# Feed-forward layers by seven block products in place of eight, with gated products through DRAM

## The chip, the cores and the metric

One core of a Trainium2 chip runs the whole program. TensorE (PE in the profile) multiplies; VectorE (DVE), ScalarE (ACT) and GpSimd (POOL) work elementwise; SyncE (SP) issues the DMAs. The metric is the device time of one execution in microseconds (us), as the median of three runs.

## The reference, cut to what matters

Two layers over a sequence of 1024 tokens with 1024 features: a mixer (RWKV-7 in layer 0, mLSTM in layer 1), each followed by a gated feed-forward network of width 2816, with modulated norms before both and a last norm behind everything.

```python
D_FF = -(-(8 * D_MODEL) // (3 * 256)) * 256      # 2816

def _swiglu(x, w_gu, w_down):
    gu = x @ w_gu
    return (jax.nn.silu(gu[..., :D_FF]) * gu[..., D_FF:]) @ w_down

    for i in range(DEPTH):
        ...
        x = x + g1 * y                            # y: the mixer
        h = _rms(x) * (1.0 + sc2) + sh2
        x = x + g2 * _swiglu(h, ffn_w_gu[i], ffn_w_down[i])
    return _rms(x) * final_w
```

## The kernel before, in words

Features lie on partitions, tokens along the free axis. The 1024 tokens are two halves of 512, so a stream is 8 tiles of 128x512 for each half: `x[0]` and `x[1]`. Every large operand is split into two parts (`split`): a rounded copy `hi` on ACT and the rest `lo = src - hi` on DVE; a product of two 128-blocks is then three matmuls (hi hi, hi lo, lo hi), each 128x128 against 128x512 (`dense`).

In a feed-forward layer `gu` makes one of 22 tiles of the gated product: 24 matmuls with the gate's weights, Silu on ACT, 24 with the up weights, a multiplication on DVE, and a split. The 22 tiles go in five groups (`GROUPS`), since SBUF does not hold all of them; after each group `down` multiplies it by its rows of the second weight matrix and adds the result, times the gate `mod`, to `x`. That is 22 x 2 x 24 x 2 + 8 x 2 x 66 = 3168 matmuls in a layer.

`ffn_open` does the first group of the first half, `ffn_rest` the others. The first half's first group runs beside the last steps of RWKV's state chain (`c` banks, one step of 64 tokens after the other), and the work of one half stands beside the norm of the other: after the projection of `x[1]` (`project`), its norm (`rstd`, `normed`) runs while PE does the rest of the first half's `down`. In layer 1 the projection of `x[0]` runs beside the last mLSTM steps. A norm is: squares on ACT, their sum on DVE, a sum over partitions on PE (`sc<-kc,mt`), a power on POOL (`rs`), a broadcast on PE (`sc<-kc,rs`), eight multiplications on DVE, eight scalings on ACT, eight splits.

All SBUF tiles of both mixers and the feed-forward layers come from one pool, `ROOM`, in which a tag has a number of rooms that the phases share. Instructions are ordered by a scheduler at build time: it puts them on each engine by priority (the program's order, moved forward by `AHEAD`) and readiness; on the chip each engine then runs its list strictly in that order. All DMAs of weights and streams are issued by SP, in one list as well, and `background` slips steps of a side task (here the second layer's modulation, `ada`) between the weights.

## Time and profile before

| | us |
|---|---|
| median of 3 runs | 3158.77 (3158.58 to 3174.7) |
| profiled execution, its span | 3153.0 |
| PE busy | 3049.4 (97%) |
| DVE busy | 1611.2 (51%) |
| ACT busy | 1231.7 (39%) |
| POOL busy | 73.8 (2%) |
| moved by DMA | 323.14 MB, 102 GB/s over the span |

The profile describes one execution, whose span is the time from the first to the last record; the median of the runs is 5.8 us above it. Inside the span stand, in order: RWKV to about 1105 us, feed-forward layer 0 to about 1860, mLSTM to about 2310, feed-forward layer 1 to 3133, and the last norm.

### The profile page before, as it was taken

To read this page: it belongs to the slowest core of one execution; us is meant where nothing else is said; L and a number is where in the kernel's file an instruction comes from. 1 tells how busy PE (TensorE), PEld (TensorE's weight loads), DVE (VectorE), ACT (ScalarE), POOL (GpSimd) and SP (SyncE) were. 2 spreads that over 40 slices of the span, in tenths; PEclk is the share of its full clock that TensorE was granted. 3 is DMA by queue.
4 is the path that set the end of the run, shared out by engine and by line. 5 is a ranking of instruction groups with operands and counts; after the bars stand their busy time and mean duration, and the time that the engine had idled before them with its cause. 6 is when DMAs were issued, how large, how long until landed. Compare 5 with 4: busy or idle time off the path is not lost.

```text
span 3153.0 us, 44874 instructions
## 1 busy us (share of the span) xinstructions
PE 3049.4 (97%) x17656; PEld 2392.0 (76%) x17656; DVE 1611.2 (51%) x3238; ACT 1231.7 (39%) x2378; POOL 73.8 (2%) x97
## 2 busy tenths in 40 slices
PE   7899989999999999999999999999999999999998
PEld 5577767777777777888888877777778888888886
DVE  7867576776577555423334276333364432323225
ACT  6656675665655633211111144323343321111112
POOL 0000000000000000000000000000000000000000
PEclk9898688999889899999999999899999999999999
DMA  8764333344444243422122151011242321111113
GB/s 293 268 213 135 100 112 111 107 115 135 137 118 123 94 133 112 127 66 82 60 84 87 54 188 57 29 46 47 67 157 93 96 76 38 58 35 60 44 44 97
DMA packets 227656, 323.14 MB, mean 102 GB/s; under 512 B 110541, under 2 KB 113229, under 8 KB 227445
## 3 DMA queue, kind: packets, MB, share of 16 engines
q1 hardware_dynamic: 213620, 295.10, 30.5%
q10 hardware_dynamic: 13824, 25.17, 2.1%
q8 instruction: 139, 2.28, 0.3%
q14 instruction: 73, 0.59, 0.1%
HBM read 268.28 MB, written 51.90 MB: 102 GB/s over the span
## 4 chain that ended last, share of the span: by engine, by line
PE 85%; DVE 6%; issue 4%; ACT 2%; DMA 1%; POOL 1%; SPq 0%; POOLq 0%; DVEq 0%; ACTq 0%
PE dn L180 42%; PE c L180 30%; PE sc L180 4%; PE iv L180 4%; PE px L180 3%; PE tr L180 1%; PE tr L616 0%; DVE wlo L185 0%; DVE a L185 0%; POOL gv L775 0%; DVE KT L249 0%; PE tr L711 0%; POOL rs L299 0%; PE tr L1078 0%; ACT whi L184 0%
## 5 line engine op out<-in xcount | busy, mean ns | idle before, releaser
L180 PE MATMUL dn<-a,whi 128*128 128x512 f32 (+2 forms) x1656 | 593.0, 427 | 18.3 <-ACT a L184 6.7
L184 ACT ACTIVATE whi<-wraw 128x1024 fp32r<-128x1024 f32 (+2 forms) x254 | 238.4, 939 | 658.6 <-PE dn L180 344.5
L185 DVE TENSOR_TENSOR wlo<-wraw,whi 128x1024 fp32r<-128x1024 f32 (+2 forms) x254 | 272.2, 1072 | 336.8 <-ACT whi L184 333.6
L180 PEld LDWEIGHTS dn<-a,whi 128*128 128x128 f32 (+2 forms) x1656 | 316.8, 197 | 102.2 <-issue 11.2
L180 PE MATMUL dn<-a,wlo 128*128 128x512 f32 (+1 forms) x856 | 362.2, 426 | 7.0 <-ACT tmp L383 2.2
L180 PEld LDWEIGHTS dn<-a,wlo 128*128 128x128 f32 (+1 forms) x856 | 168.9, 198 | 48.2 <-issue 6.9
L184 ACT ACTIVATE VU<-wraw 128x1024 fp32r<-128x1024 f32 (+2 forms) x86 | 77.2, 897 | 293.4 <-PE dn L180 131.1
L180 PE MATMUL c<-a,whi 128*128 128x512 f32 (+1 forms) x536 | 168.3, 394 | 1.1 <-DVE a L185 1.1
L185 DVE TENSOR_TENSOR VU<-wraw,VU 128x1024 fp32r<-128x1024 f32 (+2 forms) x86 | 87.7, 1020 | 120.9 <-ACT VU L184 118.8
L180 PE MATMUL dn<-AR,whi 128*128 128x512 f32 (+1 forms) x392 | 123.6, 396 | 0.0
L180 PE MATMUL dn<-KT,whi 128*128 128x512 f32 (+1 forms) x392 | 123.0, 395 | 0.0
L180 PEld LDWEIGHTS c<-a,whi 128*128 128x128 f32 (+1 forms) x536 | 100.4, 188 | 26.0 <-issue 2.2
L180 PE MATMUL c<-a,wlo 128*128 128x512 f32 x272 | 107.6, 396 | 4.2 <-ACT a L184 4.2
L824 DVE TENSOR_TENSOR tmp<-dn,tmp 128x512 f32<-128x512 f32 x46 | 31.8, 691 | 145.9 <-PE dn L180 145.9
L180 PE MATMUL c<-a,VU 128*128 128x512 f32 x408 | 99.0, 396 | 0.0
L180 PE MATMUL dn<-a,VU 128*128 128x512 f32 (+1 forms) x408 | 97.8, 395 | 0.0
L180 PEld LDWEIGHTS sc<-AR,KB 64*128 64x128 f32 x512 | 74.7, 219 | 27.7 <-issue 13.7
L180 PE MATMUL sc<-AR,KB 64*128 64x128 f32 x512 | 89.4, 320 | 2.4 <-DVE KB L575 2.0
L180 PEld LDWEIGHTS c<-a,VU 128*128 128x128 f32 x408 | 76.2, 188 | 19.1 <-issue 1.1
L180 PEld LDWEIGHTS dn<-a,VU 128*128 128x128 f32 (+1 forms) x408 | 75.4, 185 | 19.6
L756 DVE SCALAR_TENSOR_TENSOR st<-st,dl,c 64x64 f32<-64x64 f32 x256 | 71.1, 278 | 34.3 <-PE c L180 29.7
L180 PE MATMUL c<-AR,whi 128*128 128x512 f32 x280 | 88.6, 397 | 0.0
(513 smaller groups left out, 6252.2 us busy)
## 6 DMA issues: line engine op xcount, KB each, us to landing
wraw<-in_wgu SPq DMA_DIRECT2D x108, 512.0 KB, 3.5
KT<-in_ada SPq DMA_DIRECT2D x40, 512.0 KB, 5.4
wraw<-in_wdn SPq DMA_DIRECT2D x64, 256.0 KB, 2.7
wraw<-in_wdn SPq DMA_DIRECT2D x48, 320.0 KB, 2.9
eb<-in_ada SPq DMA_DIRECT2D x48, 256.0 KB, 2.9
st<-in_ada SPq DMA_DIRECT2D x48, 256.0 KB, 2.7
wraw<-in_wk SPq DMA_DIRECT2D x16, 512.0 KB, 4.5
wraw<-in_wr SPq DMA_DIRECT2D x16, 512.0 KB, 4.3
```

The source lines that it names most:

```text
L180: return self.nc.tensor.matmul(out, lhsT, rhs, start=start, stop=stop, **kw)
L184: self.nc.scalar.activation(hi, src, AF.Copy)
L185: self.nc.vector.tensor_tensor(lo, src, hi.bitcast(F32), SUB)
L756: nc.vector.scalar_tensor_tensor(st[hs, hs], st[hs, hs], dl[hs, c:c + 1], p3[hs, hs], MUL, ADD)
L824: nc.vector.tensor_tensor(sil[i], ps, sil[i], MUL)
```

## The change

Both halves and both halves of the features make 2x2 blocks, and a block product of 2x2 by 2x2 blocks is made from seven products of blocks in place of eight (Winograd's form of Strassen's scheme: four sums of blocks ahead of the products on either side, seven sums behind).

- `seven` makes two tiles (n and n + 11) for both halves: 7 x 12 = 84 matmuls where 96 stood. Nine of eleven pairs go this way for gate and up; two (`NPLAIN`) stay plain. `wpair` loads the weights of two tiles, makes four sums on POOL, and splits seven blocks on ACT and DVE. Behind the products `seven` has three copies out of PSUM on ACT and four additions on DVE.
- `keep` makes four differences of the gated tiles on DVE and writes all seven to DRAM (`gd`, 256 KB each). After the last pair, `down` reads them back, splits them, and does the second matrix in seven products of 132 matmuls, in the order 1, 6, 7, 2, 4, 5, 3. Its weights' sums are made ahead by `sums` as a side task: 16 steps in a layer, each with 4 loads, 4 POOL additions of 128x352, and 4 stores. Layer 0 asks for seven steps of the side tasks in each `wpair` (`rate` 7), layer 1 for one.
- A layer has 2 x 2 x 2 x 2 x 24 + 9 x 2 x 84 + 7 x 132 = 2820 matmuls.
- SBUF is laid out anew per phase: `ROOM` for the mixers, `FROOM` for the feed-forward layers, over each other. A tile of the new phase waits for the tiles that lay in its place. Only `x` (8 rooms, `RES`) stays.
- The order of the halves' work changes with `ffn`: norm of `x[0]`, plain tiles of the first half, projection and norm of `x[1]` (in layer 1 the projection stands ahead of the plain tiles), plain tiles of the second half, the pairs, `down`.

```diff
+NH = 11
+NPLAIN = 2
...
-AHEAD = dict(chain=50, mask=400, w=50, finish=50)
+AHEAD = dict(chain=50, mask=400, w=50, finish=50, pair=100, g=150, norm=500)
+RES = {"x": (8, 520)}
...
+FROOM = {"wraw": (3, 1024), "wq": (8, 1024), "gb": (11, 1024), "ws": (3, 512), "tmp": (4, 512), "ga": (17, 1024),
+         "tt": (8, 512), "rs": (1, 4)}
...
+    def open(self, stack, rooms):
+        self.np += 1
+        for tag, (bufs, _) in rooms.items():
+            self.pools[tag] = stack.enter_context(
+                self.tc.tile_pool(name=f"{tag}_{self.np}", bufs=bufs, reuse_waits="tile"))
+        self.rooms_.update(rooms)
+    def phase(self, rooms=None):
+        if self.big is not None:
+            self.big.close()
+            self.rooms_ = dict(RES)
+            self.pools = {n: self.pools[n] for n in RES}
+        if rooms:
+            self.big = ExitStack()
+            self.open(self.big, rooms)
...
-    def gu(self, l, n, hs, gated):
-    def down(self, l, g, gated, x, which, ns=range(KT)):
-    def ffn_open(self, l, x, hs):
-    def ffn_rest(self, l, x, hs, gated, after):
...
+    def norm_blocks(self, xs, l, which):
+        nc = self.nc
+        r = self.rstd(xs)
+        for kt in range(KT):
+            nc.vector.tensor_tensor(xs[kt], xs[kt], r, MUL)
+            nc.scalar.activation(xs[kt], xs[kt], AF.Identity, scale=self.scp[l][:, 8 * which + kt:8 * which + kt + 1],
+                                 bias=self.mod[l][:, 24 * which + kt:24 * which + kt + 1])
+    def wpair(self, s1, s2):
+        nc = self.nc
+        self.background(self.rate)
+        out = {}
+        def part(n, src):
+            out[n] = self.two("wq")
+            self.split(*out[n], src)
+        with self.ahead("pair"):
+            r1, r2 = (self.t("wraw", [P, D]) for _ in range(2))
+            nc.sync.dma_start(r1, s1)
+            nc.sync.dma_start(r2, s2)
+            a11, a12, a21, a22 = r1[:, :HT], r1[:, HT:], r2[:, :HT], r2[:, HT:]
+            u, v, w = (self.t("ws") for _ in range(3))
+            add = nc.gpsimd.tensor_tensor
+            part(1, a11)
+            part(2, a12)
+            add(u, a21, a22, ADD)
+            add(v, u, a11, SUB)
+            part(6, v)
+            part(5, u)
+            add(a21, a11, a21, SUB)
+            part(7, a21)
+            part(4, a22)
+            add(w, a12, v, SUB)
+            part(3, w)
+        return out
...
+    def seven(self, w, X, tag):
+        nc = self.nc
+        def other():
+            return self.bank(self.alt("iv", "dn", "dn"))
+        def copy(ps):
+            t = self.t(tag)
+            nc.scalar.activation(t, ps, AF.Copy)
+            return t
+        a = self.bank(self.alt("c1", "c2", "px"))
+        self.product(a, w[1], X[1])
+        c11 = copy(a)
+        b = other()
+        self.product(b, w[2], X[2])
+        nc.vector.tensor_tensor(c11, b, c11, ADD)
+        self.product(a, w[6], X[6], start=False)
+        c12 = copy(a)
+        c = other()
+        self.product(c, w[5], X[5])
+        self.product(a, w[7], X[7], start=False)
+        c21 = copy(a)
+        c22 = self.t(tag)
+        nc.vector.tensor_tensor(c22, c, c21, ADD)
+        d = other()
+        self.product(d, w[4], X[4])
+        nc.vector.tensor_tensor(c21, d, c21, ADD)
+        self.product(c, w[3], X[3], start=False)
+        nc.vector.tensor_tensor(c12, c, c12, ADD)
+        return c11, c12, c21, c22
+    def keep(self, g, n, room):
+        nc = self.nc
+        g11, g12, g21, g22 = g
+        t2, t4, t3 = room
+        def put(i, t):
+            nc.sync.dma_start(self.gd[i - 1, n], t)
+        put(1, g11)
+        put(2, g21)
+        put(3, g22)
+        nc.vector.tensor_tensor(g12, g12, g11, SUB)
+        put(5, g12)
+        nc.vector.tensor_tensor(t2, g22, g12, SUB)
+        put(6, t2)
+        nc.vector.tensor_tensor(t4, g21, t2, SUB)
+        put(4, t4)
+        nc.vector.tensor_tensor(t3, t2, g11, SUB)
+        put(7, t3)
...
+    def sums(self, l):
+        nc = self.nc
+        w = self.A["wdn"]
+        k = NH * P
+        q = k // 4
+        add = nc.gpsimd.tensor_tensor
+        for n in range(4):
+            for c in range(0, k, q):
+                a11, a21, a22, a12 = (self.t("x", [P, q]) for _ in range(4))
+                for t, m, o in ((a11, n, 0), (a21, n + 4, 0), (a22, n + 4, k), (a12, n, k)):
+                    nc.sync.dma_start(t, w[l, m, :, o + c:o + c + q])
+                s1, s2 = (self.t("x", [P, q]) for _ in range(2))
+                add(s1, a21, a22, ADD)
+                add(s2, s1, a11, SUB)
+                add(a21, a11, a21, SUB)
+                add(a12, a12, s2, SUB)
+                for i, t in enumerate((s1, s2, a21, a12)):
+                    nc.sync.dma_start(self.wsd[i, n, :, c:c + q], t)
+                yield
...
+        to = {1: ((0, 0),), 6: ((0, 1),), 7: ((1, 0), (1, 1)), 2: ((0, 0),), 4: ((1, 0),), 5: ((1, 1),), 3: ((0, 1),)}
+        ps = [None] * 4
+        for i, p in enumerate((1, 6, 7, 2, 4, 5, 3)):
+            xs = []
+            for m in range(NH):
+                with self.ahead("g"):
+                    raw = self.t("tt")
+                    nc.sync.dma_start(raw, self.gd[p - 1, m])
+                    hi, lo = self.two("gb" if i % 2 else "ga")
+                    self.split(hi, lo, raw)
+                xs.append((hi, lo))
+            fresh = p in (1, 2, 4, 5)
+            def run(n, units, lo, first, last):
+                for u, w in enumerate(units):
+                    o = lo // P + 4 * u
+                    e = o + 4 if o + 4 <= NH else NH
+                    self.product(ps[n], w, xs[o:e], start=first and u == 0 and fresh, stop=last and u == len(units) - 1)
+            for n in range(4):
+                if fresh:
+                    ps[n] = self.bank(("c1", "c2", "px", "iv")[n])
+                run(n, weights(p, n, 0, D), 0, True, False)
+                if p != 1:
+                    run(n, weights(p, n, D, k), D, False, True)
+                    self.add_to(l, x, n, ps[n], to[p])
+            if p == 1:
+                for n in range(4):
+                    run(n, weights(p, n, D, k), D, False, True)
+                    self.add_to(l, x, n, ps[n], to[p])
+            if p == 4:
+                done(0)
+        done(1)
+    def add_to(self, l, x, n, ps, to):
...
+    def ffn(self, l, x, second, done, rate):
+        nc = self.nc
+        wgu = self.A["wgu"]
+        self.store(0, x[0])
+        self.norm_blocks(x[0], l, 1)
+        b11, b21 = self.parts(x[0][:4], "gb"), self.parts(x[0][4:], "gb")
+        if l == 1:
+            second()
+        g = {}
+        for n in range(NPLAIN):
+            for m in (n, n + NH):
+                g[m, 0] = self.plain(l, m, b11 + b21)
+        self.deep = True
+        if l == 0:
+            second()
+        self.store(1, x[1])
+        self.norm_blocks(x[1], l, 1)
+        b22 = self.parts(x[1][4:7], "gb") + self.parts(x[1][7:], "ga")
+        b12 = self.parts(x[1][:4], "ga")
+        for n in range(NPLAIN):
+            for m in (n, n + NH):
+                g[m, 1] = self.plain(l, m, b12 + b22)
+            self.keep((g[n, 0], g[n, 1], g[n + NH, 0], g[n + NH, 1]), n, [self.t("tmp") for _ in range(3)])
+        for kt in range(4):
+            f11, f21, f12, f22 = x[0][kt], x[0][kt + 4], x[1][kt], x[1][kt + 4]
+            nc.vector.tensor_tensor(f12, f12, f11, SUB)
+            nc.vector.tensor_tensor(f22, f22, f12, SUB)
+            nc.vector.tensor_tensor(f21, f21, f22, SUB)
+            nc.vector.tensor_tensor(f11, f22, f11, SUB)
+        X = {1: b11, 2: b21, 3: b22, 6: self.parts(x[1][4:], "ga"), 5: self.parts(x[1][:4], "ga"),
+             7: self.parts(x[0][:4], "ga"), 4: self.parts(x[0][4:], "ga")}
+        self.rate = rate
+        for n in range(NPLAIN, NH):
+            sil = self.seven(self.wpair(wgu[l, n], wgu[l, n + NH]), X, "tt")
+            for t in sil:
+                nc.scalar.activation(t, t, AF.Silu)
+            up = self.seven(self.wpair(wgu[l, NF + n], wgu[l, NF + n + NH]), X, "tmp")
+            for t, u in zip(sil, up):
+                nc.vector.tensor_tensor(t, u, t, MUL)
+            self.keep(sil, n, up[:3])
+        self.background(1000)
+        self.rate = 0
+        x[0] = self.load(self.rooms(0), 0, self.xd[0])
+        x[1] = self.load(self.rooms(1), 1, self.xd[1])
+        self.down(l, x, done)
...
-        # the first feed-forward layer
-        self.ng = 0
-        hs = {0: self.normed(x[0], 0, 1, self.a0)}
-        gated = self.ffn_open(0, x, hs)
+        self.phase(FROOM)
+        def second(y, w, l, tag):
+            x[1] = self.load(self.rooms(1), 1, None if l == 0 else self.xd[1])
+            run(self.project(y, w, l, x[1], lambda: self.two("ga"), tag))
+        self.bg = chain(self.sums(0), *(self.ada(s, HT, RAW1, "x") for s in (1, 0, 2, 4, 3, 5)))
+        self.ffn(0, x, lambda: second(self.yd[1], "wro", 0, ("tmp",)), lambda j: self.store(j, x[j]), 7)
+        self.phase(ROOM)
         self.deep = True
-        x[1] = self.load(self.rooms(1), 1)
-        run(self.project(self.yd[1], "wro", 0, x[1], self.a1, PB))
-        hs[1] = self.normed(x[1], 0, 1, self.a1)
...
-        self.bg, self.rate = chain(*(self.ada(s, HT, RAW1, "iv") for s in (1, 0, 2, 4, 3, 5))), 1
-        self.ffn_rest(0, x, hs, gated, after)
-        self.background(48)
-        # layer 1
-        self.deep = True
+        with self.ahead("norm"):
+            nh = {0: self.normed(x[0], 1, 0, self.a0)}
         self.ml_setup()
         ml = self.mlstm(nh)
         next(ml)
+        x[1] = self.load(self.rooms(1), 1, self.xd[1])
         nh[1] = self.normed(x[1], 1, 0, self.a1)
         next(ml)
-        spill(1)
         run(ml)
-        self.ng = 0
+        self.phase(FROOM)
         self.deep = True
-        x[0] = self.load(self.rooms(0), 0, xd[0])
-        run(self.project(self.yd[0], "wmo", 1, x[0], self.a0, PT))
-        hs = {0: self.normed(x[0], 1, 1, self.a0)}
-        x[1] = self.load(self.rooms(1), 1, xd[1])
-        run(self.project(self.yd[1], "wmo", 1, x[1], self.a1, PD))
-        gated = self.ffn_open(1, x, hs)
-        hs[1] = self.normed(x[1], 1, 1, self.a1)
-        self.ffn_rest(1, x, hs, gated, lambda i: self.final(i, x[i]))
+        x[0] = self.load(self.rooms(0), 0, self.xd[0])
+        run(self.project(self.yd[0], "wmo", 1, x[0], lambda: self.two("ga"), ("tmp",)))
+        self.bg = self.sums(1)
+        self.ffn(1, x, lambda: second(self.yd[1], "wmo", 1, ("tmp",)), lambda j: self.final(j, x[j]), 1)
+        self.phase()
```

Three places show what this does to the lists. First, PE at the end of RWKV's last state chain. `c` banks are the chain's, `dn` the feed-forward layer's. Before:

```order
L180 MATMUL c_2076_11240<-st_1458,AR_10437 128x128
L180 MATMUL dn_11566<-a_11346,whi_11562 128x512
L180 MATMUL dn_11566<-a_11345,wlo_11563 128x512
L180 MATMUL dn_11566<-a_11352,whi_11562 128x512
L180 MATMUL dn_11566<-a_11353,whi_11562 128x512
L180 MATMUL dn_11566<-a_11352,wlo_11563 128x512
L180 MATMUL dn_11566<-a_11359,whi_11562 128x512
L180 MATMUL c_2077_11243<-VU_11066,KT_10494 128x128
L180 MATMUL c_2076_11240<-VU_11066,SR_10449 64x64 x2
L180 MATMUL dn_11566<-a_11360,whi_11562 128x512
L180 MATMUL dn_11566<-a_11359,wlo_11563 128x512
L180 MATMUL dn_11566<-a_11366,whi_11562 128x512
```

and now (`sc` is the norm of `x[0]`, `tr` transposes of the finished heads):

```order
L208 MATMUL c_2076_11362<-st_1580,AR_10559 128x128
L208 MATMUL c_2077_11365<-VU_11188,KT_10616 128x128
L208 MATMUL c_2076_11362<-VU_11188,SR_10571 64x64 x2
L208 MATMUL sc_11516<-kc,tmp_11493 128x1 x4
L208 MATMUL c_2078_11372<-st_1580,AR_10559 128x128
L208 MATMUL sc_11524<-kc,rs_11521 128x128 x3
L208 MATMUL c_2079_11375<-VU_11188,KT_10616 128x128
L208 MATMUL c_2078_11372<-VU_11188,SR_10571 64x64 x2
L208 MATMUL sc_11524<-kc,rs_11521 128x128
L208 MATMUL dn_11570<-gb_11545,wq_11573 128x512 x2
L814 MATMUL tr_11406<-kc,Ys_11301 128x128
```

The chain's matmuls stand alone now; the first feed-forward matmul comes behind the chain and the norm.

Second, PE at the norm of `x[1]` in feed-forward layer 0 (`sc` is the norm). Before, `c` is a bank of `down` for the first half:

```order
L180 MATMUL c_2274_12227<-SA_11592,wlo_12224 128x512
L180 MATMUL c_2274_12227<-pt_11660,whi_12223 128x512
L180 MATMUL sc_12156<-kc,mt_12133 128x1 x4
L180 MATMUL c_2274_12227<-pt_11661,whi_12223 128x512
L180 MATMUL c_2274_12227<-pt_11660,wlo_12224 128x512
L180 MATMUL sc_12164<-kc,rs_12161 128x128 x4
L180 MATMUL c_2274_12227<-pt_11729,whi_12223 128x512
L180 MATMUL c_2274_12227<-pt_11730,whi_12223 128x512
```

and now, where `dn` ends the projection and `c` begins the second half's plain tiles:

```order
L208 MATMUL dn_12111<-ga_11873,wq_12108 128x512
L208 MATMUL dn_12111<-ga_11878,wq_12107 128x512 x2
L208 MATMUL dn_12111<-ga_11878,wq_12108 128x512
L208 MATMUL sc_12168<-kc,tmp_12145 128x1 x4
L208 MATMUL sc_12176<-kc,rs_12173 128x128 x4
L208 MATMUL c_2214_12222<-ga_12209,wq_12225 128x512
L208 MATMUL c_2218_12254<-ga_12209,wq_12257 128x512
L208 MATMUL c_2214_12222<-ga_12209,wq_12225 128x512
```

What stood around the norm has moved: nothing stands now between its two products and the first matmul that reads its result. The same picture stands twice in layer 1, at the norms of `x[0]` and of `x[1]`.

Third, POOL in the pairs of feed-forward layer 0 (`ws`, `wraw`: the sums of a pair's weights; `x` with 128x352: steps of `sums`). Before, its list has only the norms' powers there. Now:

```order
L979 TENSOR_TENSOR x_12896<-x_12889,x_12890 128x352
L980 TENSOR_TENSOR x_12897<-x_12896,x_12888 128x352
L981 TENSOR_TENSOR x_12889<-x_12888,x_12889 128x352
L982 TENSOR_TENSOR x_12891<-x_12891,x_12897 128x352
L881 TENSOR_TENSOR ws_13501<-wraw_13498 128x512
L882 TENSOR_TENSOR ws_13502<-ws_13501,wraw_13497 128x512
L885 TENSOR_TENSOR wraw_13498<-wraw_13497,wraw_13498 128x512
L888 TENSOR_TENSOR ws_13503<-wraw_13497,ws_13502 128x512
L979 TENSOR_TENSOR x_12914<-x_12907,x_12908 128x352
```

The four `x` rows are one step of `sums`; three more such steps stand ahead of them, behind the last `ws` row of the pair before. So sixteen additions for `sums` have come between the additions of two pairs.

## Rows read from the trace of the kernel before

**Rows 1.** The page: the span, part 1 (engines), part 4 (chain that ended last).

```profile
span 3153.0 us, 44874 instructions
...
PE 3049.4 (97%) x17656; PEld 2392.0 (76%) x17656; DVE 1611.2 (51%) x3238; ACT 1231.7 (39%) x2378; POOL 73.8 (2%) x97
...
PE 85%; DVE 6%; issue 4%; ACT 2%; DMA 1%; POOL 1%; SPq 0%; POOLq 0%; DVEq 0%; ACTq 0%
```

**Rows 2.** Windows inside both feed-forward layers: busy per engine, PEclk, DMA share, GB/s.

```profile
1600.00:1700.00 100.00, 100.00 (x439) 81.34 (x438) 31.76 (x45) 17.64 (x26) 0.00 (x0) 1.00 0.23 71
...
2600.00:2700.00 100.00, 100.00 (x434) 81.05 (x433) 25.95 (x33) 17.53 (x26) 0.00 (x0) 1.00 0.13 39
```

**Rows 3.** Groups of instructions by line and shape.

```profile
L184 ACT ACTIVATE a<-mt 128x512 fp32r<-128x512 f32 x96 | 59.3, 622 | 7.4 <-DVE mt L375 6.1 <-ACT AR L383 0.4 <-ACT tmp L383 0.4
...
L185 DVE TENSOR_TENSOR a<-mt,a 128x512 fp32r<-128x512 f32 x96 | 65.5, 684 | 11.3 <-ACT a L184 10.6
...
L330 ACT ACTIVATE mt<-mt,mod,scp 128x512 f32<-128x512 f32 x48 | 37.2, 804 | 15.1 <-DVE mt L329 15.1
...
L837 DVE SCALAR_TENSOR_TENSOR x<-dn,mod,x 128x512 f32<-128x512 f32 x42 | 31.4, 750 | 43.2 <-PE dn L180 43.2
...
L271 DVE SCALAR_TENSOR_TENSOR iv<-eb,ca,iv 128x512 f32<-128x512 f32 x48 | 36.0, 749 | 22.4 <-DMA eb<-in_ada 21.9
```

**Rows 4.** POOL alone, groups by line and shape.

```profile
L775 POOL TENSOR_TENSOR gv<-gv,mhalf 128x8 f32<-128x8 f32 x16 | 31.5, 1968 | 468.8 <-DVE gv L774 468.8
...
L518 POOL MEMSET tmp<- 112x512 f32 x1 | 0.5, 530 | 104.8 <-PE iv L180 104.8
```

**Rows 5.** The page, part 6: DMA issues, size, time to landing.

```profile
wraw<-in_wgu SPq DMA_DIRECT2D x108, 512.0 KB, 3.5
...
wraw<-in_wdn SPq DMA_DIRECT2D x64, 256.0 KB, 2.7
```

**Rows 6.** Window in which the DMA engines moved most.

```profile
15.00:20.00 5.00, 2.65 (x11) 2.56 (x12) 1.34 (x4) 0.28 (x1) 1.88 (x1) 1.00 1.03 410
```

**Rows 7.** Timeline of PE, a step of the state chain without other matmuls between.

```profile
1019.21 0.39 PE L180 MATMUL c<-st,AR 128*128 128x128 f32 x2
...
1021.64 0.46 PE L180 MATMUL c<-st,AR 128*128 128x128 f32 x2 [0.78 <-DVE st L756]
```

**Rows 8.** Timeline of PE, the last chain: its second and its last step.

```profile
1086.99 0.38 PE L180 MATMUL c<-st,AR 128*128 128x128 f32 x2
...
1103.06 0.38 PE L180 MATMUL c<-st,AR 128*128 128x128 f32 x2
```

**Rows 9.** Window of the two last chains, PE records that write dn banks alone.

```profile
1023.00:1104.40 81.40, 45.85 (x136) 24.78 (x136) 1.38 (x2) 1.79 (x3) 0.90 0.31 99
```

**Rows 10.** Timeline of the last norm, all engines.

```profile
3138.88 1.84 PE L180 MATMUL sc<-kc,mt 128*128 128x1 f32 x8 [2.38 <-DVE mt L293]
...
3140.83 0.16 DVE L298 TENSOR_SCALAR rs<-sc 128x4 f32<-128x4 f32 x1 [2.09 <-PE sc L180]
...
3141.07 1.01 POOL L299 TENSOR_TENSOR rs<-rs,mhalf 128x4 f32<-128x4 f32 x1 [25.30 <-DVE rs L298]
...
3142.13 2.08 PE L180 MATMUL sc<-kc,rs 128*128 128x128 f32 x8 [1.41 <-POOL rs L299]
...
3144.25 5.35 DVE L1126 SCALAR_TENSOR_TENSOR SR<-SR,cc,sc 128x512 f32<-128x512 f32 x8 [3.25 <-PE sc L180]
```

**Rows 11.** Windows in the mLSTM tail where the granted clock fell.

```profile
2272.00:2276.00 4.00, 4.00 (x12) 1.93 (x11) 2.31 (x9) 0.69 (x5) 0.00 (x0) 0.50 0.27 103
...
2276.00:2280.00 4.00, 4.00 (x16) 2.98 (x16) 1.73 (x7) 0.69 (x5) 0.70 (x1) 0.50 0.00 0
...
2280.00:2284.00 4.00, 4.00 (x23) 3.18 (x22) 2.32 (x9) 1.32 (x6) 0.70 (x1) 0.79 0.18 46
```

**Rows 12.** Window of the last mLSTM chain, PE records that read a tiles alone.

```profile
2298.00:2311.60 13.60, 8.77 (x31) 5.45 (x31) 2.05 (x3) 1.50 (x3) 1.00 0.33 115
```

129 lines of the change are left out of this document (71 added, 58 removed), and 6 rows, old and new, of the table ROOM.

## The prediction

> **What bounds the kernel now.** I read the page first: PE is busy for 97% of the span, and of the chain that ended last 85% is PE [rows 1]. Then windows inside both feed-forward layers: PE has no idle time at all in 100 us, the granted clock is 1.00 (2.4 GHz), and DVE and ACT have about two thirds of their time free [rows 2]. So there a matmul less is time less, at the spacing of the window: 100 / 439 = 0.228 us in layer 0 and 100 / 434 = 0.230 us in layer 1. The question is whether the new order keeps PE that dense. I therefore read next what stands around the feed-forward layers: the end of RWKV's state chain, the norms, the end of the mLSTM.
>
> **What is removed.** 3168 - 2820 = 348 matmuls in a layer. 348 x (0.228 + 0.230) = **159 us**, the most that can be won.
>
> **What is given back at the borders.** The phases' tiles now lie over each other, and the order of the halves is another one; five places lose the work that covered them.
>
> 1. *End of RWKV.* Before, the last two chains have feed-forward matmuls between their steps: 136 records of `dn` in the 81 us to the chain's end [rows 9]. The list of the changed kernel has none there. They don't vanish, they run later: 136 x 0.228 = 31 us. The chain gets a little quicker: with this filling a step takes (1103.06 - 1086.99) / 6 = 2.68 us [rows 8], without it 1021.64 - 1019.21 = 2.43 us [rows 7]; over 16 steps 4 us come back. Behind the chain PE starts cold: the norm of `x[0]` ends only there, with eight scalings of 0.804 us on ACT, two splits of 0.622 us and the DVE part of 0.684 us [rows 3] before the second tile can be read: some 8 us, and the finish of the last heads stands between them on ACT, so 10. Together 31 - 4 + 10 = **37 us** (25 to 45: the chain without company may be quicker still, or ACT slower).
>
> 2. *Three norms without cover*: of `x[1]` in layer 0, of `x[0]` and `x[1]` in layer 1. In the lists nothing stands on PE between the norm's two products and the first matmul that reads it. The trace has one such bare norm, the last: from the sum over partitions to the first multiplication 3144.25 - 3138.88 = 5.4 us [rows 10]. Ahead of it come an addition to `x` (0.75), a square (0.62) and a sum (0.68), behind it a multiplication (0.68), eight scalings on ACT (6.4), then splits at 0.622 and one DVE part (0.68) [rows 3]. ACT's list has all eight scalings ahead of the splits, and then five splits until PE's first operand in layer 0 (the four of the lower block come first): 0.75 + 0.62 + 0.68 + 5.4 + 0.68 + 6.4 + 3.1 + 0.68 = 18.3 us. For `x[0]` in layer 1 it is nine splits, the next projection's first tile being behind the norm's eight: 20.8. For `x[1]` there, squares and sum run beside the plain tiles: 5.4 + 0.68 + 6.4 + 3.1 + 0.68 = 16.3. Together **55 us** (40, if the engines overlap better than one behind the other, to 62).
>
> 3. *End of the mLSTM.* Before, 31 matmuls of the projection stand among the last chain [rows 12], 31 x 0.230 = 7 us. Now the projection's tiles wait for rooms, a load of 256 KB (2.7 us, [rows 5]) and a split (1.3): **11 us** (5 to 18).
>
> 4. *The clock.* In the mLSTM's tail the granted clock falls to 0.50 (1.2 GHz) for two windows of 4 us, after a stretch of small matmuls, and to 0.79 in the next: 2 + 2 + 0.8 = 4.8 us lost [rows 11]. Each of the five stops above can bring that; I take half, **12 us** (0 to 24). The Trainium skill (TensorE: Matmul & The Clock Gate, section "Why this matters for your kernels") says that idle gaps between matmul bursts drop the engine to half its clock; the trace agrees as far as rows 11 go, where the engine was busy with little. By that rule every stop pays, and the term would be 24 us in place of 12.
>
> 5. *Starts of `down` and of the mLSTM.* The last pair's tiles hold the rooms that `down`'s first products and the mLSTM's first tiles need. Some of each is ready early (the products of the last seven free their operands one after the other, 12 x 0.229 = 2.7 us apart). **8 us** for four borders (0 to 25).
>
> **What the pairs cost.** A seven is 84 x 0.229 = 19.2 us of PE. ACT has seven splits and three copies of 0.62 us (6.2) and half of four Silus; DVE seven splits, four additions, and half of four products and four differences, 15 x 0.684 = 10.3 us [rows 3]. Both stay under 19.2. A bank is copied by ACT while PE does another product of 2.7 us, so 0.62 us is covered unless ACT is more than 2 us behind; I take 0.2 us for each of 36 sevens, **7 us** (0 to 36).
>
> POOL's large addition does not occur before. The nearest rows are a memset of 112x512, 0.53 us, and a power of 128x8, 1.97 us [rows 4], which is another operation, and DVE's 0.684 for two inputs. An addition cannot well be quicker than the memset, which only writes; upwards nothing in the trace bounds it. I take twice the memset, 1.1 us (0.76 for 128x352). A pair's weights need 4.4 of 19.2 us, so POOL is not the bound. Worst is layer 0: all 16 steps of `sums` come with the first sets of weights, once four steps between two sets: 16 x 0.76 = 12 us, and 2.7 us each for a load and a store where they aren't hidden, 12 to 34 us in all, against a lead of about one seven. SP's list puts stores of gated tiles and weights behind `x` loads that wait for POOL. **10 us** (0 to 40). Layer 1, with one step for each set, costs nothing: 4 x 0.76 = 3 us of POOL beside 19.2 of PE. `down` reads 11 x 256 KB and 2.9 MB of weights in 132 x 0.229 = 30 us, some 190 GB/s; the trace has 410 GB/s in a window [rows 6], so it is hidden.
>
> **The sum.** 37 + 55 + 11 + 12 + 8 + 7 + 10 = 140 us back of 159: the span becomes 3153 - 19 = 3134, and with the 5.8 us by which the median stood above the profiled span, **3139 us**, 0.6% less.
>
> **The rivals.**
> - *The borders cost only their lower bounds, and the pairs nothing.* 25 + 40 + 5 = 70 us back: 3153 - 89 + 5.8 = 3069; with a little of each, up to 3105. For it: ACT and DVE have much free time [rows 2]. Against: the norms are chains of one engine behind the other. Chance 0.27.
> - *GpSimd becomes the bound in layer 0* (slower than before). The first seven sets of weights hold 28 additions of 128x512 and 64 of 128x352, worth 72 of the former, in 7 x 19.2 = 135 us: from 1.9 us for one POOL is the bound, at 2.5 us 180 us are needed, 45 more, and the result is 3139 + 35 = 3174; at 3 us 3139 + 71 = 3210, more if layer 1 follows (116 additions' worth in 346 us: also from 3.0). For it: POOL's power of 8 columns takes 1.97 us [rows 4]. Against: its memset moves 512 columns in 0.53. Chance 0.13. The Trainium skill (GPSIMD Engine Reference, section "Elementwise — side-by-side cycle accounting") gives GpSimd's two-input addition 1.96 times VectorE's time, which from the 0.684 of the trace would be an estimate of 1.3 us; by that this rival would not happen and the sum would stay.
> - *VectorE and GpSimd take turns.* If a two-input operation on one stops the other, the first seven sets in layer 0 need 10.3 + 4.4 + 7 = 21.7 us each, 2.5 more than PE: 17 us more, 3156. The rows of before can't show it, POOL being idle. Chance 0.1. The same page of the Trainium skill, GPSIMD Engine Reference, section "Specifications", says that the two share their way into SBUF when VectorE has two inputs there.
> - *Every seven waits 1 to 2 us* for a copy, a split or a room: 36 x 1.5 = 54, less the 7 counted: 3186. Chance 0.1.
> - That the saving itself fails has no place: the matmuls are gone from the list.
>
> **The numbers.** My forecast has 0.4, with 3105 to 3165 as its own range. Under 0.5% (16 us) the measurement can hardly tell from no change. Faster by more than that (below 3143): 0.27 and 0.28 of my case's 0.4, 0.55. Within: 0.1 of mine, the turns, and a share of the waits, 0.24. Slower (above 3174): GpSimd and most of the waits, 0.21. The range, 3085 to 3195, leaves out 0.1 on either side.
>
> **What would show it.** The profile after should have PE idle at the end of RWKV (no `dn` among the last 16 steps), three gaps of 16 to 21 us before matmuls whose releaser is ACT or DVE splits, and windows inside the pairs at 100% with DVE near half. A POOL addition over 1.9 us, or PE idle in the pairs behind PSUM copies, would make it wrong to the slow side; norm gaps under 12 us, to the fast side.

## The result, and the profile after

The changed kernel takes **3210.31 us** (median of 4 runs, 3195.53 to 3217.21) against 3158.68 for the kernel before beside it: 1.0143 times, 95% interval 1.0102 to 1.0184. I had forecast 3139 with 3085 to 3195, so it went the wrong way and out of the range.

The page of the changed kernel, which answers to [rows 1]: the span, and part 1 with its matmuls.

```profile
span 3214.2 us, 46353 instructions
PE 2946.6 (92%) x16960; PEld 2318.8 (72%) x16960; DVE 1950.4 (61%) x3736; ACT 1437.8 (45%) x2815; POOL 428.8 (13%) x369
```

The 696 matmuls are gone, as the change says (17656 to 16960), but PE is busy 92% where it was 97%. Windows of 50 us show where. Behind the name of a window stand its length, then busy time (and instructions) of PE, weight loads, DVE, ACT and POOL, the granted clock, the DMA share and GB/s; a full window of `down` or of the plain tiles holds 222 matmuls, one of the pairs 217 to 230; [rows 2] come to 219.5 and 217.

```profile
1200.00:1250.00 50.00, 36.57 (x154) 29.81 (x153) 28.47 (x42) 20.19 (x29) 1.01 (x1) 0.83 0.26 90
...
1300.00:1350.00 50.00, 43.44 (x173) 34.68 (x173) 30.94 (x31) 13.62 (x24) 34.88 (x28) 0.91 0.63 204
1350.00:1400.00 50.00, 27.68 (x108) 22.02 (x107) 15.21 (x18) 9.30 (x16) 25.99 (x25) 0.75 0.66 213
1400.00:1450.00 50.00, 35.13 (x138) 28.01 (x137) 26.15 (x27) 11.50 (x21) 30.66 (x24) 0.83 0.66 226
...
1700.00:1750.00 50.00, 50.00 (x222) 41.14 (x221) 32.00 (x51) 25.54 (x45) 0.00 (x0) 1.00 0.75 248
...
2350.00:2400.00 50.00, 41.57 (x189) 32.45 (x188) 27.30 (x57) 19.14 (x45) 3.49 (x5) 0.89 0.62 207
2400.00:2450.00 50.00, 40.10 (x156) 32.06 (x155) 28.17 (x40) 22.36 (x34) 1.01 (x1) 0.83 0.44 145
...
2500.00:2550.00 50.00, 38.48 (x167) 31.60 (x166) 21.51 (x29) 18.48 (x26) 1.96 (x1) 0.85 0.28 95
...
2700.00:2750.00 50.00, 35.88 (x143) 27.84 (x141) 22.20 (x27) 10.87 (x20) 30.48 (x26) 0.93 0.63 205
```

Three of them (1200, 2400, 2500) are the bare norms, 2350 is the end of the mLSTM, and `down` (1700) is full, as forecast. What was not forecast are the windows *inside* the pairs, 1300 to 1450 and 2600 to 2800, and these have one thing in common: POOL is busy for 24 to 35 of 50 us, so steps of `sums` run there. Over all windows of the pairs PE is idle for 62 us in layer 0 (1250 to 1700) and 29 in layer 1 (2550 to 2800); by missing matmuls, which takes in the lower clock, it is 77 and 42.

How a step of `sums` comes to stop PE is seen in PE's longest wait in the pairs of layer 0 (us in total, times, longest) and in timelines of ACT, POOL and SP in the same 30 us (start, duration, engine, line, tiles; in brackets the idle time before it and what ended it; `wsd<-x` are a step's stores, `x<-in_wdn` the next step's loads):

```profile
PE c L208 <- ACT tmp L911: 26.1, 2, 22.3
```

```profile
1360.59 0.62 ACT L212 ACTIVATE wq<-wraw 128x512 fp32r<-128x512 f32 x1
1387.94 1.15 ACT L212 ACTIVATE wq<-ws 128x512 fp32r<-128x512 f32 x2 [26.73 <-POOL ws L882]
1389.00 0.58 ACT L911 ACTIVATE tmp<-c 128x512 f32<-128x512 f32 x1
```

```profile
1363.99 0.94 POOL L979 TENSOR_TENSOR x<-x,x 128x352 f32<-128x352 f32 x1 [5.52 <-DMA gd<-tt]
...
1373.17 0.93 POOL L979 TENSOR_TENSOR x<-x,x 128x352 f32<-128x352 f32 x1 [5.42 <-issue]
...
1381.65 0.93 POOL L979 TENSOR_TENSOR x<-x,x 128x352 f32<-128x352 f32 x1 [4.79 <-DMA x<-in_wdn]
...
1385.30 1.26 POOL L881 TENSOR_TENSOR ws<-wraw 128x512 f32<-128x512 f32 x1
1386.65 1.26 POOL L882 TENSOR_TENSOR ws<-ws,wraw 128x512 f32<-128x512 f32 x1
```

```profile
1374.12 3.09 SPq L984 DMA_DIRECT2D wsd<-x  x4
1377.26 1.86 SPq L977 DMA_DIRECT2D x<-in_wdn  x4
1379.22 0.38 SPq L875 DMA_DIRECT2D wraw<-in_wgu  x1
```

Read it from the end. PE waits for the copy of a bank (L911 at 1389.00) for 22.3 us. The product that is copied has long been done, but the copy stands in ACT's list behind the split of a pair's weights, which waits 26.73 us for POOL's second addition (L882). POOL does that at once when it comes to it, but ahead of it in its list stand four steps of `sums` in a row, 8.5 to 10 us apart: some 4 us of additions and 4 to 5.5 us of idle time for loads, since SP's list holds a step's stores, which wait for POOL, ahead of the next step's loads. The same holds for the pair itself: the load of the second half of its weights (L875) stands in SP's list behind these steps and is issued only at 1379.22. Such a load lands 3.7 us after its issue (the median on the page), so POOL's addition at 1385.30 could have come some 2 us sooner with nothing else ahead of it in POOL's list, not more. Lists in order have passed a delay of the least urgent work on to the most urgent, over SP and three engines.

### The profile page after: what moved, and what is told of

The parts are those of the page before. It is cut to its first block, busy times and chain, and to the rows that moved or that the text cites. A ratio compares the mean times of both kernels' runs of the same rounds, so it can differ in the third digit from the quotient of the medians.

```text
span 3214.2 us, 46353 instructions
## 1 busy us (share of the span) xinstructions
PE 2946.6 (92%) x16960; PEld 2318.8 (72%) x16960; DVE 1950.4 (61%) x3736; ACT 1437.8 (45%) x2815; POOL 428.8 (13%) x369
## 5 line engine op out<-in xcount | busy, mean ns | idle before, releaser
L208 PE MATMUL c<-ga,wq 128*128 128x512 f32 x1998 | 490.3, 400 | 53.2 <-ACT tmp L911 32.5
L212 ACT ACTIVATE wq<-wraw 128x512 fp32r<-128x512 f32 (+2 forms) x368 | 248.3, 678 | 584.1 <-PE c L208 265.4
L208 PEld LDWEIGHTS c<-ga,wq 128*128 128x128 f32 x1998 | 382.5, 193 | 142.6 <-ACT tmp L911 37.3
L213 DVE TENSOR_TENSOR wq<-wraw,wq 128x512 fp32r<-128x512 f32 (+2 forms) x368 | 304.6, 833 | 283.7 <-ACT wq L212 280.0
L208 PE MATMUL dn<-a,whi 128*128 128x512 f32 (+2 forms) x1048 | 401.9, 449 | 17.4 <-ACT a L212 6.2
L208 PE MATMUL c<-gb,wq 128*128 128x512 f32 x1014 | 248.0, 398 | 4.5 <-DVE tt L926 2.3
L208 PE MATMUL dn<-a,wlo 128*128 128x512 f32 (+2 forms) x552 | 244.0, 446 | 7.1 <-ACT tmp L416 2.2
L208 PE MATMUL dn<-ga,wq 128*128 128x512 f32 x894 | 224.3, 400 | 14.9 <-ACT ga L212 11.1
L208 PEld LDWEIGHTS c<-gb,wq 128*128 128x128 f32 x1014 | 192.9, 192 | 49.1 <-DVE tt L926 3.9
L208 PEld LDWEIGHTS dn<-ga,wq 128*128 128x128 f32 x894 | 173.3, 195 | 54.2 <-ACT ga L212 12.1
```

Of the source, the lines that this page charges most:

```text
L208: return self.nc.tensor.matmul(out, lhsT, rhs, start=start, stop=stop, **kw)
L212: self.nc.scalar.activation(hi, src, AF.Copy)
L213: self.nc.vector.tensor_tensor(lo, src, hi.bitcast(F32), SUB)
```

## The experiments

Theory: `sums` costs what was lost in the pairs, through the lists it shares. Rivals: the pairs wait by themselves, or GpSimd's slow additions or its traffic do it. e1 to e5 are one run each; the four runs of the change lie 22 us apart, so smaller differences between them say little.

**e1_no_sums** leaves the sums out (`down` reads plain blocks in their place, four of its products then having other factors).

```diff
-            return self.wsd[{5: 0, 6: 1, 7: 2, 3: 3}[p], n]
+            return A["wdn"][l, n + 4 * (p % 2)][:, (p > 5) * k:(p > 5) * k + k]
-        self.bg = chain(self.sums(0), *(
+        self.bg = chain(*(
-        self.bg = self.sums(1)
+        self.bg = iter(())
```

> Leaves out the side task that sums the second matrix's blocks, in both layers; down reads plain blocks of that matrix in their place, as many bytes, so the products 5, 6, 7 and 3 have wrong factors. Theory (the steps of sums hold up the pairs, through SP's and POOL's lists): most of the loss inside the pairs goes, 77 us in layer 0 and 41 us in layer 1 become under 25 together, so 3216 - 95 = 3120 us (3095 to 3140). Rival (the pairs wait by themselves, for PSUM copies, rooms or the additions on their own weights): above 3185. Rival (VectorE and GpSimd take turns): the pairs' own additions stay, so about half of the loss, 3155 to 3175.

3117.87 us. Its windows in the pairs of both layers:

```profile
1300.00:1350.00 50.00, 42.45 (x181) 33.90 (x181) 46.86 (x65) 14.81 (x25) 13.86 (x9) 0.93 0.74 241
...
1500.00:1550.00 50.00, 50.00 (x230) 41.63 (x229) 26.87 (x40) 17.80 (x30) 15.51 (x11) 1.00 0.33 110
...
2650.00:2700.00 50.00, 50.00 (x220) 40.90 (x219) 29.27 (x42) 18.33 (x31) 14.30 (x11) 1.00 0.35 120
```

Without sums the pairs are full in layer 1, and in layer 0 from 1500 on, with POOL's own additions for them (14 of 50 us) still in place. The sums cost 3210 - 3118 = 92 us. What is left in layer 0, 14 us of idle time on PE from 1300 to 1500, is the stretch in which the modulation's loads and VectorE's work for it run.

**e2_stores_pool** issues the sums' stores from GpSimd (L984, `nc.sync` to `nc.gpsimd`), which frees SP's list.

> The stores of sums are issued by POOL, right behind the additions that make them, in place of SP; everything else stays. If SP's list is what is held up (a store waits there for an addition, and weights and gated tiles wait behind it): 3150 to 3180 us. If POOL's list is it (a pair's additions behind the additions of several steps): above 3200, since POOL's list is the same or longer.

3231.09 us, not faster: POOL is now busy for 44.7 of the 50 us from 1300 on, and PE for 30. The wait left SP's list and the work came into POOL's, which was the one that was late.

**e3_sums_dve** and **e4_pair_dve** move additions to VectorE: e3 those of the sums, e4 those of the pairs.

```diff
 def sums  (e3)
-        add = nc.gpsimd.tensor_tensor
+        add = nc.vector.tensor_tensor
 def wpair (e4)
-            add = nc.gpsimd.tensor_tensor
+            add = nc.vector.tensor_tensor
```

> The 64 additions of sums in each layer run on DVE in place of POOL (about 0.5 us each for 352 columns, 32 us of DVE per layer). If POOL's list is what holds the pairs up: 3130 to 3165 us. If it is SP's list: the stores still wait for additions there, which come sooner; 3175 to 3205. If VectorE's load is the limit, it gets slower than 3216.

> The four additions of each seven's weights run on DVE in place of POOL (2.8 us of DVE per seven); sums stay on POOL. If the pairs wait because their additions stand behind the additions of sums in POOL's list: 3130 to 3160 us. If the weights themselves are loaded late (SP's list): above 3190. If VectorE's load is the limit, slower than 3216.

3133.85 us for e3, 0.8% less than before beside it: 76 of the 92 us are back. 3199.55 for e4, within the spread of the change's own runs, with PE still at 36, 39 and 35 of 50 us from 1300 on. So it is not enough that the pairs' additions get out of POOL's list: VectorE, which now makes them, waits 36 us in five pieces for the pairs' weights (1250 to 1500). The steps themselves have to be quick, since SP's list holds the pairs' loads and the gated stores behind them. e3 makes them quick and empties POOL's list at once; it doesn't say which of the two gave how much.

**e5_own_lists** puts all of the sums (loads, additions, stores) into POOL's list, and the pairs' additions on VectorE.

```diff
-                    nc.sync.dma_start(t, w[l, m, :, o + c:o + c + q])
+                    nc.gpsimd.dma_start(t, w[l, m, :, o + c:o + c + q])
-                    nc.sync.dma_start(self.wsd[i, n, :, c:c + q], t)
+                    nc.gpsimd.dma_start(self.wsd[i, n, :, c:c + q], t)
```

> The sums of the `down` blocks move whole into GpSimd's list (their loads, additions and stores), and the pairs' own additions go to VectorE, so that neither SP's list nor the pairs stand behind a step of the sums. Theory (the sums delay the pairs through the in-order lists they share): about 3125 us (3110 to 3150), PE near 50 of 50 us in the windows of the pairs. Rival (the sums' traffic or GpSimd's access to SBUF slows the others, whoever issues it): stays near 3190, with PE at 35 to 40 of 50 us in 1300 to 1450.

3243.91 us. By its time the expectation failed. Its windows, its groups on POOL and what VectorE waits for (us in total, times, longest), all of 1200 to 1700 but the groups, say how:

```profile
1300.00:1350.00 50.00, 48.33 (x212) 39.12 (x211) 33.80 (x50) 18.32 (x31) 35.88 (x50) 1.00 0.67 226
1350.00:1400.00 50.00, 47.82 (x209) 38.79 (x208) 35.37 (x47) 17.75 (x30) 35.71 (x49) 1.00 0.62 206
1400.00:1450.00 50.00, 14.90 (x66) 12.01 (x64) 6.22 (x9) 6.09 (x11) 37.94 (x58) 0.69 0.46 155
```

```profile
L984 POOL DMA_DIRECT2D wsd<-x x128 | 69.4, 548 | 0.0
L977 POOL DMA_DIRECT2D x<-in_wdn x128 | 69.1, 546 | 71.6 <-ACT ga L212 69.5 <-issue 2.1
```

```profile
DVE x L301 <- DMA x<-in_ada: 59.7, 2, 58.5
```

For 100 us the sums run beside the pairs, POOL 36 of 50 us busy and 206 to 226 GB/s on the way, and PE stands at 48 of 50. So the traffic, as much as in the change, does not slow the pairs; nor does GpSimd's work at this rate, which is 37 us of additions in the 100 (61 in the change from 1300 to 1400, with the pairs' own), the rest being issues. But each issue takes POOL 0.55 us, a step now takes 10 to 15 us, and the sums are not done when the modulation's rows want a load into the `x` tiles, which both use: VectorE waits 58.5 us for it in one piece, and PE 66.3 behind VectorE. That the rooms of `x` are what held that load I argue from the code.

**e9_prefetch** loads a step's blocks before the additions and stores of the step ahead of it; the sums are made in place, so that two steps fit into the eight rooms.

```diff
                 for t, m, o in ((a11, n, 0), (a21, n + 4, 0), (a22, n + 4, k), (a12, n, k)):
                     nc.sync.dma_start(t, w[l, m, :, o + c:o + c + q])
-                s1, s2 = (self.t("x", [P, q]) for _ in range(2))
-                add(s1, a21, a22, ADD)
...
+                if last:
+                    finish(*last)
+                last = n, c, a11, a21, a22, a12
```

> The changed kernel with one edit: each step of the sums loads the blocks of the next step before it adds and stores its own (the sums are made in place, so that two steps fit in the eight rooms). The additions stay on GpSimd. Theory (a step is slow because its load, its additions and its stores follow one another through SP's and GpSimd's lists): a step falls from 9 or 10 us to 5 or 6, PE in 1300 to 1450 rises from 28 to 35 of 50 us to above 42, and the time falls to 3160 us (3140 to 3180). Rival (GpSimd's addition itself is what costs): 3200 to 3215.

3170.64 us (1.0011 times before, 0.998 to 1.0042), 40 less than the change. The first additions of successive steps on POOL (L976 here):

```profile
1339.62 0.92 POOL L976 TENSOR_TENSOR x<-x,x 128x352 f32<-128x352 f32 x1 [0.41 <-DMA x<-in_wdn]
1344.96 0.92 POOL L976 TENSOR_TENSOR x<-x,x 128x352 f32<-128x352 f32 x1 [1.42 <-DMA wsd<-x]
1349.26 0.92 POOL L976 TENSOR_TENSOR x<-x,x 128x352 f32<-128x352 f32 x1 [0.36 <-DMA x<-in_wdn]
```

A step takes 4.3 to 5.4 us in these rows in place of 9, with the same additions on the same engine. (The edit did two things for this, the order of the loads and the rooms for two steps; they aren't told apart.) PE from 1300 to 1400 did not rise above 42, as I had expected, but stands at 35 and 27 of 50: eleven steps now pass in a row between the additions for two pairs, from 1306 to 1363. The gain lies behind it: in the windows of the pairs PE is idle for some 51 us in place of 62 in layer 0, and for 11 in place of 29 in layer 1.

**e12_spread** lets a step of the sums alternate with six steps of the modulation in layer 0, so that POOL's list has one step for each set.

```diff
-        self.bg = chain(self.sums(0), *(self.ada(s, HT, RAW1, "x") for s in (1, 0, 2, 4, 3, 5)))
+        def mix():
+            a = chain(*(self.ada(s, HT, RAW1, "x") for s in (1, 0, 2, 4, 3, 5)))
+            for _ in self.sums(0):
+                yield
+                for _ in range(6):
+                    next(a, None)
+                    yield
+            yield from a
+        self.bg = mix()
```

> The changed kernel with one edit in layer 0: a step of the sums alternates with six steps of the modulation's side work, so that GpSimd's list has one step for each set of weights there, and not two to five. Layer 1 is unchanged. Theory (bunches of steps hold up the sets, a set waiting for as many serial steps as stand ahead of it): 35 to 50 of the some 77 us lost in layer 0's pairs come back, 3165 us (3155 to 3180). Rival (each step costs its 4 to 5 us wherever it stands): 3200 to 3215.

3180.26 us (1.0053 times before, 1.0022 to 1.0083), 30 less than the change: at the slow edge of what bunching gives and 20 below the rival's 3200, so bunching is a part of it. PE is at 42 to 47 of 50 us from 1300 to 1550, nowhere at 28, and at 39 to 45 in layer 1, which was left alone:

```profile
1350.00:1400.00 50.00, 44.66 (x192) 35.75 (x192) 37.67 (x49) 14.62 (x25) 26.84 (x21) 0.97 0.72 237
```

For what is left the rival has its part: with one step between them (once two) sets still stand 24 us apart (1318.36 to 1629.62 in 13 distances), where e1, without steps, has 22 beside the modulation and 20 behind it. By these two traces a step costs 2 to 4 us even by itself.

**e6_norms** puts, with e3's edit, the other half's tiles between a norm and its first reader: in layer 1 `second()` comes before the norm of `x[0]`, in layer 0 between the plain tiles, and the norms are written with the priority of `ahead("norm")`.

```diff
+        if l == 1:
+            second()
         self.store(0, x[0])
-        self.norm_blocks(x[0], l, 1)
-        b11, b21 = self.parts(x[0][:4], "gb"), self.parts(x[0][4:], "gb")
-        if l == 1:
-            second()
+        with self.ahead("norm"):
+            self.norm_blocks(x[0], l, 1)
+            b11, b21 = self.parts(x[0][:4], "gb"), self.parts(x[0][4:], "gb")
         g = {}
         for n in range(NPLAIN):
+            if l == 0 and n == 1:
+                self.deep = True
+                second()
...
-        self.deep = True
-        if l == 0:
-            second()
         self.store(1, x[1])
-        self.norm_blocks(x[1], l, 1)
+        with self.ahead("norm"):
+            self.norm_blocks(x[1], l, 1)
```

**e7_rate4** is e6 with rate 4 in place of 7 (72 of layer 0's 112 side steps then stand beside pairs, the others behind them). **e8_warm** is e6 with 184 matmuls that nothing reads, at the end of RWKV:

```diff
         self.chunks(x[0])
+        d = self.t("a", dt=F32R)
+        nc.scalar.activation(d, self.k_("scan"), AF.Copy)
+        for _ in range(46):
+            ps = self.bank("dn")
+            for q in range(4):
+                self.mm(ps, d[:, :P], d, start=q == 0, stop=q == 3)
```

> The sums' additions are on VectorE as in the run before that had this alone (3134 us), and the second pair's or plain tiles' matmuls stand between a norm's products and their first reader. Theory (the three bare norms cost 13 to 15 us each in that run): 3134 - 3 x 15 = 3089 us (3080 to 3105). Rival (the norms' work on ACT and DVE delays the tiles that now cover it, so that the wait only moves): 3115 to 3135.

> As e6_norms, with the sums and the rest of layer 0's side work spread thinner: four steps where there were seven. Theory (the rest of the idle time inside layer 0's pairs is side work in bunches): 10 to 15 us below e6_norms. Rival (it is the pairs' own chain of loads, additions and splits): the same as e6_norms within 5 us.

> As e6_norms, with 184 matmuls added that nothing reads, between the last steps of RWKV's chain, where the kernel before had the matmuls of `down`. Theory (without filling the granted clock stays at 0.50 there and a step takes 2.95 us; with it the clock rises and a step takes 2.7 us or less): the chain ends about 12 us earlier, and the time is 5 to 12 us below e6_norms. Rival (the chain is bound by latencies of ACT and DVE, whatever the clock): no gain, or 5 to 20 us more for the matmuls that stand in its way.

3093.05 us for e6 (0.9774, 0.9719 to 0.9828): 41 less than the one run of e3, so three bare norms cost some 14 us each, and the cover holds. Its windows at 1200, 2350 and 2400 have PE at 49 of 50 us. 3115.17 for e7, the theory missed: spreading by the rate gains nothing. 3088.5 for e8 (0.9761, 0.9709 to 0.9814), not to be told from e6 by its time.

**e10_prefetch_dve**, **e11_prefetch_pool** (e8 with early loads, additions on VectorE and on GpSimd), **e13_spread_dve**, **e14_spread_early** (e8 with e12's order, without and with early loads), **e15_spread_cold** (e13 without the added matmuls).

> e8_warm with the same early loads; the sums' additions are on VectorE. Theory (what is left in layer 0's pairs is VectorE at the head of its list waiting 15 us for the sums' loads): 10 to 20 us less than e8_warm's 3088, some 3073. Rival (the DMA engines, 85% busy there, are the bound): the same within 5 us.

> As e10_prefetch_dve, but with the sums' additions on GpSimd, as the change had them. Theory (with the loads early GpSimd is no longer late): within 10 us of e10_prefetch_dve. Rival (GpSimd's 1.1 to 1.5 us for an addition still delays the pairs): 20 to 50 us more than e10_prefetch_dve.

> e8_warm with the same spreading in layer 0. Theory (bunching): 10 to 20 us below e8_warm's 3088, some 3073. Rival (what is left there is the modulation's loads and VectorE's work, which stay): 3085 to 3095.

> e13_spread_dve with the early loads. Theory (early loads hurt in e10 only because the sums' loads and stores then came in a bunch and held up the pairs' weights): within 5 us of e13_spread_dve or up to 10 less, so 3065 to 3078. Rival (the early loads hurt by themselves, the rooms being fewer for the others): 20 to 30 us more than e13_spread_dve.

> e13_spread_dve without the added matmuls at the end of RWKV's chain. Theory (they pay by keeping the clock up): 8 to 15 us more than e13_spread_dve. Rival (they cost as much as they give): the same within 4 us.

e10 3116.19 (0.9849, 0.9814 to 0.9884) and e11 3125.42 us (0.9894, 0.9833 to 0.9956): theory missed for e10, whose early loads make e8 28 us slower. A window of e10, and the first addition of a pair on POOL in it:

```profile
1300.00:1350.00 50.00, 31.14 (x123) 24.48 (x122) 29.86 (x53) 7.10 (x12) 5.45 (x4) 0.80 0.88 285
```

```profile
1333.20 1.26 POOL L881 TENSOR_TENSOR ws<-wraw 128x512 f32<-128x512 f32 x1 [58.96 <-DMA wraw<-in_wgu]
```

The sums now run so fast that a pair's weights come late behind them: POOL waits 59 us for a load of `wraw`, which SP issues only at 1327.83, behind ten steps' loads and stores; the DMA engines are 88% busy (e8: 82%). Spread out (e14), the early loads cost no more than the runs can tell: 3104.68 against e13's 3097.15, ranges overlapping. In e14's trace successive sets are at most 25 us apart, in e10's once 73, so the bunch is what stopped PE there. By the times alone e14 and e10 are not told apart either (0.9772 to 0.9835 against 0.9814 to 0.9884), so that bunching is all of e10's loss is not shown. e11 against e10 (9 us, intervals overlapping): with early loads it matters little which engine adds. e13 itself (0.9785, 0.9753 to 0.9818) is no faster than e8, the theory missed: once VectorE adds, spreading gains nothing that the runs can tell.

e15 takes 3097.94 us, the same as e13. But their traces differ where the matmuls were added. DVE writes the state `st` at each step: the first rows of each fence are the same step (the one behind a long gap), the next ones the last step; then the window of 1050. First e13, then e15:

```profile
806.55 0.57 DVE L789 SCALAR_TENSOR_TENSOR st<-st,dl,c 64x64 f32<-64x64 f32 x2 [0.81 <-PE c L208]
...
1111.06 0.59 DVE L789 SCALAR_TENSOR_TENSOR st<-st,dl,c 64x64 f32<-64x64 f32 x2 [0.64 <-PE c L208]
...
1050.00:1100.00 50.00, 49.01 (x493) 38.81 (x492) 23.30 (x58) 28.21 (x73) 2.61 (x2) 0.97 0.15 42
```

```profile
810.66 0.57 DVE L789 SCALAR_TENSOR_TENSOR st<-st,dl,c 64x64 f32<-64x64 f32 x2 [0.69 <-PE c L208]
...
1119.26 0.59 DVE L789 SCALAR_TENSOR_TENSOR st<-st,dl,c 64x64 f32<-64x64 f32 x2 [0.89 <-PE c L208]
...
1050.00:1100.00 50.00, 39.35 (x385) 31.43 (x384) 18.45 (x47) 23.41 (x65) 3.00 (x2) 0.50 0.26 73
```

With the filling the clock is 0.97 and not 0.50, and the last steps come 2.4 us apart (1108.65, 1111.06) in place of 2.95 (1116.31, 1119.26). From the marked step to the last one it is 1111.06 - 806.55 = 304.5 us with the filling and 1119.26 - 810.66 = 308.6 without, so the chain gains 4 us. To the end of the span it is 3080.0 - 806.55 = 2273 and 3098.1 - 810.66 = 2287, but the trace of e13 is that of its fastest execution. So the clock effect is shown in the traces; that it pays over many runs is not: runs of one kernel lie up to 34 us apart.

## Why the prediction was wrong

From the same step to the end the kernel before takes 3153.0 - 805.92 = 2347 us and the changed one 3214.2 - 814.25 = 2400, 53 more; the 8 us before that step belong to the execution, since all kernels do the same work there (it falls between 800 and 826 us in the runs). The rows, of before and after:

```profile
805.92 0.57 DVE L756 SCALAR_TENSOR_TENSOR st<-st,dl,c 64x64 f32<-64x64 f32 x2 [0.66 <-PE c L180]
...
1106.06 0.29 DVE L756 SCALAR_TENSOR_TENSOR st<-st,dl,c 64x64 f32<-64x64 f32 x1
```

```profile
814.25 0.57 DVE L789 SCALAR_TENSOR_TENSOR st<-st,dl,c 64x64 f32<-64x64 f32 x2 [0.81 <-PE c L208]
...
1122.04 0.59 DVE L789 SCALAR_TENSOR_TENSOR st<-st,dl,c 64x64 f32<-64x64 f32 x2 [2.50 <-PE c L208]
...
1133.37 0.80 PE L208 MATMUL dn<-gb,wq 128*128 128x512 f32 x1 [10.02 <-ACT gb L212]
```

- **The saving** (159 us) holds: the matmuls are gone, at nearly the same spacing (50 / 222 = 0.225 us).
- **The 10 us (0 to 40) for POOL's and SP's lists, with "Layer 1, with one step for each set, costs nothing": the step that failed.** It cost 92 us (e1, one run). The price of a step was not far off: 4 x 0.76 and 2.7 each way, 8.5 us, against 9 measured, and of the 34 us that I had as the bound for four steps, four took 31 (1353.85 to 1385.30). I misread how often it happens. POOL's list has four, two, five, two and three steps between the first sets of layer 0, not four once. In layer 1 the program asks for one step with each set, but the list has two or three between the first ones. The first additions of successive sets in layer 1 of the changed kernel:

```profile
2635.39 1.50 POOL L881 TENSOR_TENSOR ws<-wraw 128x512 f32<-128x512 f32 x1 [4.89 <-DMA wraw<-in_wgu]
...
2663.69 1.28 POOL L881 TENSOR_TENSOR ws<-wraw 128x512 f32<-128x512 f32 x1
...
2687.80 1.29 POOL L881 TENSOR_TENSOR ws<-wraw 128x512 f32<-128x512 f32 x1 [3.39 <-DMA wraw<-in_wgu]
...
2835.19 1.29 POOL L881 TENSOR_TENSOR ws<-wraw 128x512 f32<-128x512 f32 x1 [9.64 <-DVE wq L213]
...
2852.91 1.29 POOL L881 TENSOR_TENSOR ws<-wraw 128x512 f32<-128x512 f32 x1 [8.12 <-DMA wraw<-in_wgu]
```

  With two or three steps between them sets are 24 to 28 us apart, without steps 17 to 21, about PE's own 19.2. I had set one step's additions (3 us) against 19.2, when it was two steps' *serial* time, 18 us, plus the set's own additions of 6 (1.41 to 1.53 us each, where I had 1.1). And a lead of one set gives way once, not a dozen times.
- **"End of RWKV", 37 us,** was mis-sized: 31 for the moved matmuls stands as worked out, no run having it by itself, and the start behind the chain took 11.3 (1133.37 - 1122.04) for my 10, but the chain does not get 4 us quicker, it gets 8 longer (1122.04 - 814.25 = 308 against 1106.06 - 805.92 = 300): without filling the clock falls to 0.50 and a step takes 2.95 us (e15), not the 2.43 of [rows 7], where the clock had not yet fallen. Some 50 us.
- **"Three norms without cover", 55 us,** is right in kind and within its bounds: by missing matmuls 68, 66 and 55 times 0.225, so 43 us with their share of clock; 41 by e6.
- **"End of the mLSTM", 11 us:** PE is idle for 8.4 us in 2350 to 2400. The 12 us of clock lie within these rows, and the starts of `down` (8) cost nothing that shows. [rows 11] are no stop of PE: it has no idle time there (4.00 of 4.00 us), and the clock fell all the same, so they don't bear out what I set beside them. At stops it fell too: the windows of the norms have 0.83 to 0.85, with 10 to 13 us of idle time in each.
- **The rivals.** The time is that of GpSimd as the bound at 3 us an addition, but by chance: the additions stay under the 1.9 us from which that decides. What fills POOL's time between two sets is additions and the waits for loads in one series. VectorE and GpSimd do slow each other (last section), but e1, with the pairs' own additions still on GpSimd, is full in the pairs of layer 1; so neither that nor a wait of every seven was the loss. Without the sums the change would have won 42 us (e1 against 3160 beside it), where my sum has 29 without its 10 for these lists.

With 50 + 43 + 8 and 91 (idle time) to 119 (missing matmuls) for the pairs, 192 to 220 come back from 159: 33 to 61 more, and 53 were measured.

## What to carry to other kernels

Work off the critical path has a price through the lists it stands in. Count, list by list, what stands ahead of the urgent instruction, how often, and for how long in series (load, work, store), not how busy the engine is. Here the scheme gave most when its side work was on the engine that has time and its borders were covered: e8 and e13, at 2.4 and 2.2% less than before (intervals from 1.8 to 2.9%), are the same seven products with three and four placements changed. Making side work quicker can hurt as well, when it then goes ahead in a bunch.
